# Six of 22 k-pairs by seven products in each down column pair of a decoder layer, not five

## The chip, the cores and the metric

The kernel runs on one core of one Trainium2 chip. The metric is the device time of one execution in microseconds (us). Before the change three runs took 1735.93, 1736.4 and 1738.6 us; the median is 1736.4. Below, PE is the tensor engine, DVE the vector engine, ACT the scalar engine, POOL the GpSimd engine and SP the engine that issues the weight transfers.

## The reference, cut to what matters

One decoder layer over 256 tokens of width 2048 in float32: a feed-forward block (FFN), a mixing block (gated linear attention beside dilated attention), and a second FFN. Nearly all the work is in matrix products with weights.

```python
def swiglu(x, w_gate, w_up, w_down):
    return (jax.nn.silu(x @ w_gate) * (x @ w_up)) @ w_down

x = x + 0.5 * swiglu(rms_norm(x, ffn1_norm), ffn1_w_gate, ffn1_w_up, ffn1_w_down)   # D_FF = 5632
h = rms_norm(x, mix_norm);  z = h @ w_in
...
x = x + jnp.concatenate([o_g, o_a], axis=-1) @ w_out
x = x + 0.5 * swiglu(rms_norm(x, ffn2_norm), ffn2_w_gate, ffn2_w_up, ffn2_w_down)
```

The change concerns the product with `w_down` in both FFNs: 256 tokens by 5632, times 5632 by 2048.

## The kernel before

**Products.** A float32 product is made of three matmuls in a faster format. Each operand is split into a high and a low part (`split`, L111 to L114: ACT copies to the high part `wh`, `hh` or `uh`, DVE subtracts to get `wl`, `hl` or `ul`), and PE adds high by high, high by low and low by high (L274, L276, L278). Stationary is a 128x128 block of activations, moving are 512 columns of weights.

**The down stage.** Its 5632 rows of weights are 44 k-tiles of 128, or 22 k-pairs. Its 2048 columns are two column pairs (`cp` 0 and 1) of 2 x 512. A column pair is one call of `seven_pair`, which walks 22 k-pairs in the order of a string in `DOWN_ORDERS`: `s` is a k-pair done plainly, `g` a k-pair done by seven products. A plain k-pair is two k-tiles x two token halves x two column halves x 3 matmuls = 24 matmuls. A `g` treats token halves, k-tiles and column halves as a 2x2 block product and needs seven block products instead of eight: 21 matmuls (`seven_products`, L298 to L300). `g`s take the k-pairs 0, 1, 2, ... and `s`s the rest. The two FFNs and the gate and up stages before them use the same functions; the last gate and up block, b = 10, is a plain `column_pair`.

**What a `g` needs beside its matmuls.** Of activations: a *form* (`seven_forms`, L316 to L322 and a split), four sums of blocks, made once per FFN and used in both column pairs. Forms lie in parts of `hh` and `hl`, the normed input of the gate and up stages, which are free by then (`dforms`). Of weights: `seven` prepares four parts in order, "plain", "last", "sums" and "more". "plain" first adds rows into `room["sum"]` (L238), which in the down stage is the tile `urs`, and splits the middle of the raw weights. "last" is a half-size split into `hl`. "sums" adds twice in place (L246) and splits `urs`. "more" splits what L246 made, and frees the raw tile.

**Who else uses `urs`.** The gate and up stages end in 11 column blocks; the result of each is transposed in 32x32 pieces by DVE (`us`) and moved by POOL into `urs` in 16 small transfers for each token half (`move_squares`, L133). `finish()` then splits `urs` into `uh` and `ul`, the activations of the down stage. L238 of the first `g` writes `urs`, so it comes behind the `finish()` of block 10.

**Order and buffers.** `weights()` prepares two tiles ahead of PE; there are four `wh`/`wl` buffers and three raw buffers of 1 MB, each filled by one SP transfer. Side work waits in the list `later` and is run a few items a step by `run_later`, spread over `span` steps; a plain k-tile has two steps, a `g` none. The tile framework then orders instructions engine by engine with a schedule of its own; each engine runs its list in order.

**Norm blocks.** `done(t, c, blk)` of the first FFN is `renorm`, which puts into `later` the norm of one block of 512 columns. For c < 2 this is `norm_moved`: DVE transposes, POOL moves 16 pieces into `hh[:, i:i+2]` with i = 8 + 2 * (2 * c + t), and `finish` is held (`held`, `holding`) until the last `g` of the second column pair, because it writes `hh` and `hl` 0 to 7, where forms lie.

Of the kernel before, what the change touches and what calls it, by code (L numbers as in the profile page):

```python
# [38 lines left out]
def _order(text):  # L39

    seven, plain = iter(range(text.count("g"))), iter(range(text.count("g"), len(text)))
    return [(next(seven), True) if c == "g" else (next(plain), False) for c in text]


FF_ORDERS = [_order("ssgssgss" if b in FF_SEVEN else "ssssssss") for b in range(FF // 512)]
DOWN_ORDERS = [_order("ssssssgssgssgssgssgsss"), _order("sgsssgssgsssgssgssssss")]


def layer_kernel(tc, x, xT, gains, gla_gate_up, gla_gate_bias, gla_out_norm, att_q_norm, att_k_norm,
# [6 lines left out]
    with ExitStack() as es:  # L56
# [14 lines left out]
        def four_banks(odd):  # L71

            if odd:
                return [paux.tile([P, 512], F32, name="acc", tag="acc") for _ in range(2)] + [tp_bank() for _ in range(2)]
            return [pacc.tile([P, 512], F32, name="acc", tag="acc") for _ in range(4)]
# [17 lines left out]
        hh = cst.tile([P, KT, S], F32R, name="hh")  # L93
        hl = cst.tile([P, KT, S], F32R, name="hl")
# [66 lines left out]
        def stat_block(t, c):  # L161
            nc.scalar.activation(junk, xs[:, t, c * 512:(c + 1) * 512], AF.Square, accum_out=ss[:, t, c:c + 1])
# [10 lines left out]
        def jobs_of(w, orders):  # L173
            for cp, order in enumerate(orders):
                for kp, seven in order:
                    for part in ("plain", "last", "sums", "more") if seven else (0, 1):
                        yield w, cp * len(order) + kp, part

        jobs = [*jobs_of(w_ff1, FF_ORDERS), *jobs_of(w_dn1, DOWN_ORDERS)]
        jobs += [(w_mix, i, k) for i in range(3 * KT // 2) for k in range(2)] + ["low"]  # L180
        jobs += [(w_mix, i, k) for i in range(3 * KT // 2, 3 * KT) for k in range(2)]
        jobs += [(w_out, i, k) for i in range(w_out.shape[0]) for k in range(2)]
        jobs += [*jobs_of(w_ff2, FF_ORDERS), *jobs_of(w_dn2, DOWN_ORDERS)]

# [69 lines left out]
        def weights(early=False):  # L254
            if early:
                return prepare()
            while jobs and len(ready) <= AHEAD:
                prepare()
            return ready.pop(0)

        def alt(a):

            return a.rearrange("p (b a) -> p a b", b=2)
# [4 lines left out]
        def products(ps, t, acts, ws, first, last, js=((0, 1),)):  # L268
            for jj in js:
                for i, ((ah, al, k), (wh, wl)) in enumerate(zip(acts, ws)):  # L270
                    sh = ah[:, k, t * P:(t + 1) * P]
                    sl = al[:, k, t * P:(t + 1) * P]
                    for j in jj:
                        nc.tensor.matmul(ps[j], lhsT=sh, rhs=alt(wh[:, j, :]), start=first and i == 0, stop=False)  # L274
                    for j in jj:
                        nc.tensor.matmul(ps[j], lhsT=sh, rhs=alt(wl[:, j, :]), start=False, stop=False)  # L276
                    for j in jj:
                        nc.tensor.matmul(ps[j], lhsT=sl, rhs=alt(wh[:, j, :]), start=False, stop=last and i == len(ws) - 1)  # L278

        later = []  # L280
        held, holding = [], [0]

        def run_later(n):
            for _ in range(min(n, len(later))):
                later.pop(0)()

        def seven_products(cs, ms, acts, forms, first, last):

            tok = [slice(t * P, (t + 1) * P) for t in range(NT)]
            a11, a12, a22 = [[a[:, acts[k][2], tok[t]] for a in acts[k][:2]] for t, k in ((0, 0), (0, 1), (1, 1))]
            s1, s3, s2, sa = [[f[:, i, :] for f in forms] for i in range(4)]

            def product(bank, a, ws, j, start, stop):
                nc.tensor.matmul(bank, lhsT=a[0], rhs=alt(ws[0][:, j, :]), start=start, stop=False)  # L298
                nc.tensor.matmul(bank, lhsT=a[0], rhs=alt(ws[1][:, j, :]), start=False, stop=False)  # L299
                nc.tensor.matmul(bank, lhsT=a[1], rhs=alt(ws[0][:, j, :]), start=False, stop=stop)  # L300

            ws = weights()
            product(ms[0], a11, ws, 0, first, last)
            product(cs[0], sa, ws, 1, False, False)
            product(cs[1], a12, weights(), 0, False, False)
            ws = weights()
            product(ms[1], s1, ws, 0, first, last)
            product(ms[3], s3, ws, 1, first, last)
            ws = weights()
            product(ms[2], s2, ws, 0, first, last)  # L310
            product(cs[3], a22, ws, 1, False, False)
# [13 lines left out]
        def seven_pair(acts, pairs, forms, odd, evac, fold, span=None, final=False):  # L325

            cs, ms, folds = four_banks(odd), None, []
            order[0] = 4 * (1 - odd)
            units = [u for kp, seven in pairs for u in ([kp] if seven else [(2 * kp,), (2 * kp + 1,)])]
            lastseven = max(n for n, u in enumerate(units) if not isinstance(u, tuple))  # L330
            steps = span or 2 * sum(isinstance(u, tuple) for u in units)
            total = done = step = n = 0
            while n < len(units):
                u = units[n]
                if isinstance(u, tuple):
                    g = WBUF if final and n == len(units) - WBUF else 1
                    ws = [weights() for _ in range(g)]
                    last = n + g == len(units)
                    for t in range(NT):
                        step += 1  # L340
                        total = max(total, done + len(later))
                        go = min(max(-(-total * min(step, steps) // steps) - done, 0), len(later))
                        done += go
                        run_later(go)
                        if folds:
                            folds.pop(0)()
                        now = [acts[v[0]] for v in units[n:n + g]]
                        products(cs[2 * t:2 * t + 2], t, now, ws, n == 0, last, ((0,), (1,)) if g > 1 else ((0, 1),))
                        if last:
                            evac(t, [c.rearrange("p (a b) -> p b a", b=2) for c in cs[2 * t:2 * t + 2]])  # L350
                    n += g
                    continue
                start = ms is None
                if start:
                    ms = four_banks(1 - odd)
                seven_products(cs, ms, acts[2 * u:2 * u + 2], forms[u], start, n == lastseven)
                if n == lastseven:
                    folds = fold([m.rearrange("p (a b) -> p b a", b=2) for m in ms])
                    if holding[0] == 1:
                        later.extend(held)  # L360
                        held.clear()
                        holding[0] = total = done = step = 0
                        steps = 2 * (len(units) - n) - 6
                n += 1
# [36 lines left out]
        def ffn(name, done, extra=None, final=False):  # L401
            with tc.tile_pool(name=name, bufs=1, reuse_waits="tile") as fp:
# [67 lines left out]
                def lent(a, k, i):  # L470
                    return a[:, k:k + 2, :].rearrange("p k (t q) -> p (k t) q", q=P) if i else a[:, k:k + 2, :].rearrange("p k s -> p (k s)").unsqueeze(1)

                rooms["down"] = {"sum": urs, "wh": lent(hl, 8, 0), "wl": lent(hl, 10, 0)}
                dforms = {kp: [lent(hh, 2 * kp, 1), lent(hl, 2 * kp, 1)] for kp in range(4)}
                dforms[4] = [lent(hl, 12, 1), lent(hl, 14, 1)]
                for kp in range(5):
                    later.insert(min(2 * kp + 1, len(later)), lambda kp=kp: seven_forms(dacts[2 * kp:2 * kp + 2], dforms[kp], t512("full"), t512("sums")))
                for cp in range(2):
                    def evac(t, ps, cp=cp):
# [18 lines left out]
                    holding[0] = NT - cp  # L498
                    seven_pair(dacts, DOWN_ORDERS[cp], dforms, cp, evac, fold, span=28 if cp else 20, final=final and cp == 1)
                spare.close()  # L500
# [23 lines left out]

        def renorm(t, c, gi):

            later.append(lambda: (norm_moved if c < 2 else norm_block)(t, c, gi))
            later.append(lambda: stat_block(t, c))
            if c == 3:
                later.append(lambda: norm_finish(t))  # L530

# [384 lines left out]
```

## Time and profile before

| what | value |
|---|---|
| median of three runs | 1736.4 us |
| the profiled execution, its own time | 1736.26 us |
| its span, first to last instruction | 1734.5 us |
| DVE busy | 1299.5 us (75%) |
| ACT busy | 921.3 us (53%) |
| POOL busy | 438.9 us (25%) |
| mean granted clock | 1.00 |
| weights' transfers of the down stages | 88 of 1 MB, 4.8 us from issue to landing (median) |
| POOL transfers into `urs` | 704 of 16 KB, 3.6 us from issue to landing (median) |

Times in the profile are us from the first instruction. In the first FFN block 10 of the gate and up stage ends on PE at about 457 us and the down stage runs to about 680 us; in the second FFN it runs from about 1509 us to the end. In a timeline row the columns are start, duration, engine, line, operation, what is written <- what is read, count, and in brackets the idle time before it with what ended it.

### The profile page before, as it was taken

What the parts mean: (1) busy time and instruction counts of PE and PEld (TensorE: products, weight loads), DVE (VectorE), ACT (ScalarE), POOL (GpSimd) and SP (SyncE); (2) the same over time, 40 slices, a digit from 0 to 9 for tenths busy, and PEclk for the clock granted to TensorE, in tenths of its full rate; (3) what the DMA queues carried; (4) which work ended last, traced back from release to release, by engine and by line L of the source; (5) the groups of instructions that cost most, each with busy time, mean ns of one, the idle gap of its engine ahead of it and who ended that gap; (6) DMA issues with size and microseconds to landing.
All of it is one profiled execution on the core that took longest, in us unless ns stands there. A gap on an engine that the chain in (4) does not pass through costs nothing.

```text
span 1734.5 us, 22127 instructions
## 1 busy us (share of the span) xinstructions
PE 1725.2 (99%) x8100; PEld 1503.4 (87%) x8100; DVE 1299.5 (75%) x1535; ACT 921.3 (53%) x1142; POOL 438.9 (25%) x870
## 2 busy tenths in 40 slices
PE   9999999999999999999999999999999999999999
PEld 7888888888888888888888888888888888888887
DVE  7788888855788787566655658688888965687875
ACT  7555555544555554565754545455555544455453
POOL 0333334444300601011000033333333343320000
PEclk9999999999999999999999999999999999999999
DMA  8666566666656656555444465556666666655653
GB/s 341 219 221 228 207 215 224 234 221 220 209 201 222 209 216 241 194 195 210 161 170 161 155 207 186 226 209 234 224 225 223 219 216 223 209 211 210 232 213 137
DMA packets 80846, 367.59 MB, mean 212 GB/s; under 512 B 19249, under 2 KB 36657, under 8 KB 38497
## 3 DMA queue, kind: packets, MB, share of 16 engines
q1 hardware_dynamic: 50864, 350.25, 55.9%
q0 software_dynamic: 29152, 14.87, 3.4%
q8 instruction: 63, 1.03, 0.2%
q10 hardware_dynamic: 720, 1.07, 0.2%
q14 instruction: 47, 0.38, 0.1%
HBM read 350.38 MB, written 2.10 MB: 203 GB/s over the span
## 4 chain that ended last, share of the span: by engine, by line
PE 82%; DVE 9%; DMA 5%; issue 2%; ACT 1%; POOL 1%; SPq 0%; DVEq 0%; ACTq 0%
PE acc L276 20%; PE acc L278 20%; PE acc L274 20%; DVE wl L114 4%; DMA raw<-in_w_ff_dram 4%; PE tp L278 3%; PE tp L276 3%; PE tp L274 3%; PE acc L300 2%; PE acc L299 2%; PE acc L298 2%; ACT wh L113 1%; DVE raw L246 1%; DMA urs<-us 1%; DVE t L238 1%
## 5 line engine op out<-in xcount | busy, mean ns | idle before, releaser
L114 DVE TENSOR_TENSOR wl<-raw,wh 128x1024 fp32r<-128x1024 f32 (+1 forms) x658 | 793.3, 1218 | 302.9 <-ACT wh L113 299.4
L113 ACT ACTIVATE wh<-raw 128x1024 fp32r<-128x1024 f32 (+1 forms) x660 | 682.2, 1048 | 562.5 <-PE acc L278 337.0
L133 POOL DMA_DIRECT2D urs<-us x704 | 344.3, 497 | 551.9 <-issue 287.6
L276 PE MATMUL acc<-wl,hh 128*128 128x512 f32 x1376 | 416.6, 381 | 0.4 <-DVE wl L114 0.4
L278 PE MATMUL acc<-wh,hl 128*128 128x512 f32 x1376 | 414.6, 380 | 0.0
L274 PE MATMUL acc<-wh,hh 128*128 128x512 f32 x1376 | 409.2, 381 | 1.6 <-ACT wh L113 1.6
L274 PEld LDWEIGHTS acc<-wh,hh 128*128 128x128 f32 x1376 | 259.5, 189 | 39.3 <-ACT wh L113 2.7
L276 PEld LDWEIGHTS acc<-wl,hh 128*128 128x128 f32 x1376 | 259.4, 189 | 38.6 <-DVE wl L114 1.5
L278 PEld LDWEIGHTS acc<-wh,hl 128*128 128x128 f32 x1376 | 259.6, 189 | 36.5
L276 PE MATMUL acc<-wl,uh 128*128 128x512 f32 x408 | 122.8, 379 | 0.0
L278 PE MATMUL acc<-wh,ul 128*128 128x512 f32 x408 | 122.5, 379 | 0.0
L274 PE MATMUL acc<-wh,uh 128*128 128x512 f32 x408 | 119.6, 379 | 0.2 <-ACT wh L113 0.2
L133 POOL DMA_DIRECT2D hh<-us x128 | 62.2, 508 | 158.9 <-issue 133.5
L274 PEld LDWEIGHTS acc<-wh,uh 128*128 128x128 f32 x408 | 77.0, 189 | 11.6 <-ACT wh L113 0.6
L278 PEld LDWEIGHTS acc<-wh,ul 128*128 128x128 f32 x408 | 77.1, 189 | 11.0
L276 PEld LDWEIGHTS acc<-wl,uh 128*128 128x128 f32 x408 | 77.1, 189 | 10.9
L165 POOL TENSOR_TENSOR rs<-a,mhalf 128x4 f32<-128x4 f32 (+1 forms) x12 | 17.4, 1454 | 256.8 <-DVE a L592 256.8
L274 PE MATMUL tp<-wh,hh 128*128 128x512 f32 x192 | 58.6, 379 | 0.0
L278 PE MATMUL tp<-wh,hl 128*128 128x512 f32 x192 | 57.1, 379 | 0.0
L276 PE MATMUL tp<-wl,hh 128*128 128x512 f32 x192 | 57.1, 379 | 0.0
L238 DVE TENSOR_TENSOR t<-raw 128x1024 f32<-128x1024 f32 x28 | 33.8, 1207 | 25.6 <-DMA raw<-in_w_ff_dram 25.6
L113 ACT ACTIVATE wh<-t 128x1024 fp32r<-128x1024 f32 x28 | 29.5, 1054 | 39.7 <-DVE t L238 33.0
(273 smaller groups left out, 1994.8 us busy)
## 6 DMA issues: line engine op xcount, KB each, us to landing
raw<-in_w_ff_dram SPq DMA_DIRECT2D x175, 1024.0 KB, 5.0
raw<-in_w_dn_dram SPq DMA_DIRECT2D x88, 1024.0 KB, 4.8
raw<-in_w_mix_dram SPq DMA_DIRECT2D x48, 1024.0 KB, 4.7
raw<-in_w_out_dram SPq DMA_DIRECT2D x16, 1024.0 KB, 4.8
urs<-us POOLq DMA_DIRECT2D x704, 16.0 KB, 3.6
xs<-in_x_dram SPq DMA_DIRECT2D x2, 1024.0 KB, 9.7
hh<-us POOLq DMA_DIRECT2D x128, 16.0 KB, 3.4
xt<-in_xT_dram SPq DMA_DIRECT2D x7, 256.0 KB, 6.6
```

The lines of the kernel that those rows point to most:

```text
L113: nc.scalar.activation(dst_h, src, AF.Copy)
L114: nc.vector.tensor_sub(dst_l, src, dst_h.bitcast(F32))
L133: nc.gpsimd.dma_start(dst[32 * q:32 * q + 32, r * P:(r + 1) * P], src[32 * r:32 * r + 32, q * P:(q + 1) * P])
L165: nc.gpsimd.tensor_tensor(dst, src, mhalf[:, :src.shape[-1]], op=ALU.pow)
L238: nc.vector.tensor_add(room["sum"], b1, mid)
L246: nc.vector.tensor_add(raw[:, 1, j, :], b, raw[:, 1, j, :])
L274: nc.tensor.matmul(ps[j], lhsT=sh, rhs=alt(wh[:, j, :]), start=first and i == 0, stop=False)
L276: nc.tensor.matmul(ps[j], lhsT=sh, rhs=alt(wl[:, j, :]), start=False, stop=False)
L278: nc.tensor.matmul(ps[j], lhsT=sl, rhs=alt(wh[:, j, :]), start=False, stop=last and i == len(ws) - 1)
L298: nc.tensor.matmul(bank, lhsT=a[0], rhs=alt(ws[0][:, j, :]), start=start, stop=False)
L299: nc.tensor.matmul(bank, lhsT=a[0], rhs=alt(ws[1][:, j, :]), start=False, stop=False)
L300: nc.tensor.matmul(bank, lhsT=a[1], rhs=alt(ws[0][:, j, :]), start=False, stop=stop)
```

## The change

Each string of `DOWN_ORDERS` gets a sixth `g`. In the first column pair the first `g` moves from the seventh place to the fifth, and the last two `g`s have one `s` between them instead of two. In the second column pair three spacings of two `s`s and one of one `s` follow the first wide one. There is a sixth form; forms 1 to 4 take the room of the old forms 0 to 3, form 5 that of the old form 4, and form 0 lies in `hh` 12 to 15, where `norm_moved` of c = 1 wants to put its moved block. So the norm and statistics blocks of c = 1 go to a list `second` and join `later` only after the first `g` of the second column pair, the last reader of form 0.

```diff
-DOWN_ORDERS = [_order("ssssssgssgssgssgssgsss"), _order("sgsssgssgsssgssgssssss")]
+DOWN_ORDERS = [_order("ssssgssgssgssgssgsgsss"), _order("sgsssgssgssgssgsgsssss")]
...
         later = []
+        second = []
...
                 seven_products(cs, ms, acts[2 * u:2 * u + 2], forms[u], start, n == lastseven)
+                if start:
+                    later.extend(second)
+                    second.clear()
...
-                dforms = {kp: [lent(hh, 2 * kp, 1), lent(hl, 2 * kp, 1)] for kp in range(4)}
-                dforms[4] = [lent(hl, 12, 1), lent(hl, 14, 1)]
-                for kp in range(5):
+                dforms = {kp + 1: [lent(hh, 2 * kp, 1), lent(hl, 2 * kp, 1)] for kp in range(4)}
+                dforms[0] = [lent(hh, 12, 1), lent(hh, 14, 1)]
+                dforms[5] = [lent(hl, 12, 1), lent(hl, 14, 1)]
+                for kp in range(6):
                     later.insert(min(2 * kp + 1, len(later)), lambda kp=kp: seven_forms(...))
...
-            later.append(lambda: (norm_moved if c < 2 else norm_block)(t, c, gi))
-            later.append(lambda: stat_block(t, c))
+            to = second if c == 1 and holding[0] else later
+            to.append(lambda: (norm_moved if c < 2 else norm_block)(t, c, gi))
+            to.append(lambda: stat_block(t, c))
```

Lines from L281 on stand 1 to 6 numbers later in the changed kernel (L316 is L317, L320 L321, and so on); L114, L238 and L246 keep theirs.

How the lists of the engines change is shown at two places. The first is the way into the first `g` of the first column pair in the first FFN. On PE the 24 matmuls of each of two plain k-pairs no longer stand before it. On DVE this stood before; `full`, `sums` and the splits of `sums` belong to forms, `wl` to weight tiles, the `ul` row is the `finish()` of the second token half of block 10, and the row with `urs<-raw` is the first instruction of the `g` that needs `urs`:

```order
L320 TENSOR_TENSOR sums<-full 128x128
L321 SCALAR_TENSOR_TENSOR sums<-sums,full 128x128
L114 TENSOR_TENSOR wl<-raw,wh 128x1024
L322 TENSOR_TENSOR sums<-full,sums 128x128
L114 TENSOR_TENSOR hl<-sums,hh 128x512
L114 TENSOR_TENSOR hl<-sums,hl 128x512
L114 TENSOR_TENSOR ul_2980<-urs,uh_2979 128x4x128
L238 TENSOR_TENSOR urs<-raw 128x1024
L246 TENSOR_TENSOR raw<-urs,raw 128x512
L246 TENSOR_TENSOR raw<-raw 128x512
L114 TENSOR_TENSOR wl<-urs,wh 128x1024
```

And this stands there in the changed kernel:

```order
L317 TENSOR_TENSOR full<-uh,ul 128x256 x2
L321 TENSOR_TENSOR sums<-full 128x128
L320 TENSOR_TENSOR sums<-full 128x128
L114 TENSOR_TENSOR hl<-sums,hh 128x512
L322 SCALAR_TENSOR_TENSOR sums<-sums,full 128x128
L323 TENSOR_TENSOR sums<-full,sums 128x128
L114 TENSOR_TENSOR hl<-sums,hl 128x512
L114 TENSOR_TENSOR ul_2980<-urs,uh_2979 128x4x128
L238 TENSOR_TENSOR urs<-raw 128x1024
L246 TENSOR_TENSOR raw<-urs,raw 128x512
L246 TENSOR_TENSOR raw<-raw 128x512
L114 TENSOR_TENSOR wl<-urs,wh 128x1024
```

The end of the list is the same, `ul`, L238, twice L246, split of `urs`; all six forms still stand ahead of it, and four splits of weight tiles no longer do. On ACT the same place read, before, with `uh` for the two `finish()`es and `wh<-urs` for the part "sums":

```order
L113 ACTIVATE wh<-raw 128x1024 x2
L113 ACTIVATE hh<-sums 128x512
L113 ACTIVATE hl<-raw 128x512
L113 ACTIVATE wh<-raw 128x1024
L113 ACTIVATE uh_2979<-urs 128x4x128
L113 ACTIVATE wh<-raw 128x1024 x2
L113 ACTIVATE hh<-sums 128x512
L113 ACTIVATE hl<-sums 128x512
L113 ACTIVATE uh_2979<-urs 128x4x128
L113 ACTIVATE wh<-urs 128x1024
```

And in the changed kernel:

```order
L113 ACTIVATE wh<-raw 128x1024
L113 ACTIVATE hl<-raw 128x512
L113 ACTIVATE wh<-raw 128x1024 x3
L113 ACTIVATE hh<-sums 128x512 x2
L113 ACTIVATE uh_2979<-urs 128x4x128
L113 ACTIVATE hh<-sums 128x512 x2
L113 ACTIVATE hl<-sums 128x512
L113 ACTIVATE uh_2979<-urs 128x4x128
L113 ACTIVATE wh<-urs 128x1024
```

No weight tile is split any more between the two `finish()`es; the forms and both `finish()`es stand ahead of `wh<-urs`, as they did.

The second place is the last two `g`s of the second column pair in the first FFN. On DVE, before, with `hf` and `hl<-hf` for the held norm blocks:

```order
L238 TENSOR_TENSOR urs<-raw 128x1024
L114 TENSOR_TENSOR wl<-raw,wh 128x1024
L114 TENSOR_TENSOR hl<-raw,hl 128x512
L114 TENSOR_TENSOR hl<-hf,hh 128x4x128
L114 TENSOR_TENSOR wl<-raw,wh 128x1024
L153 TENSOR_TENSOR hf<-hh,gT 128x512
L114 TENSOR_TENSOR wl<-raw,wh 128x1024
L114 TENSOR_TENSOR hl<-hf,hh 128x4x128
L246 TENSOR_TENSOR raw<-urs,raw 128x512
L114 TENSOR_TENSOR wl<-urs,wh 128x1024
L246 TENSOR_TENSOR raw<-raw 128x512
L114 TENSOR_TENSOR wl<-raw,wh 128x1024 x2
```

And in the changed kernel, from the "sums" of the fifth `g` to that of the sixth:

```order
L114 TENSOR_TENSOR wl<-urs,wh 128x1024
L153 TENSOR_TENSOR hf<-hh,gT 128x512
L238 TENSOR_TENSOR urs<-raw 128x1024
L114 TENSOR_TENSOR wl<-raw,wh 128x1024 x3
L114 TENSOR_TENSOR hl<-raw,hl 128x512
L114 TENSOR_TENSOR hl<-hf,hh 128x4x128
L114 TENSOR_TENSOR wl<-raw,wh 128x1024
L114 TENSOR_TENSOR hl<-hf,hh 128x4x128
L246 TENSOR_TENSOR raw<-urs,raw 128x512
L114 TENSOR_TENSOR wl<-urs,wh 128x1024
L246 TENSOR_TENSOR raw<-raw 128x512
L114 TENSOR_TENSOR wl<-raw,wh 128x1024 x2
```

L238 of the sixth `g` now stands ahead of the fifth's last split, and the two last held splits stand inside the sixth `g`.

## The prediction

> **What bounds the kernel now.** I read the page first: busy shares and granted clock.
>
> ```profile
> PE 1725.2 (99%) x8100; PEld 1503.4 (87%) x8100; DVE 1299.5 (75%) x1535; ACT 921.3 (53%) x1142; POOL 438.9 (25%) x870
> PEclk9999999999999999999999999999999999999999
> ```
>
> PE is busy in 1725.2 of 1734.5 us at full clock: every matmul taken away is a gain, and every wait of PE is a loss, one for one. So the second view is the list of what PE waits for (total us, times, longest).
>
> ```profile
> PE acc L274 <- ACT wh L113: 1.9, 2, 1.6
> PE tp L102 <- DVE warm L99: 1.5, 1, 1.5
> PE tp L298 <- ACT wh L113: 0.7, 2, 0.5
> PE acc L298 <- ACT wh L113: 0.6, 1, 0.6
> ```
>
> Nothing else is above 0.4 us. The two largest waits are at the program's start; the L298 rows are `g`s that found their weights up to 0.6 us late. DVE, 75% busy, is the engine that can make PE wait, so the third view is busy time by stretches of the down stage of the first FFN (columns: window, length, PE, PEld, DVE, ACT, POOL, clock, DMA share, GB/s).
>
> ```profile
> 461.10:484.80 23.70, 23.70 (x112) 20.75 (x111) 22.89 (x47) 13.70 (x17) 13.70 (x29) 1.00 0.66 229
> 490.00:577.00 87.00, 87.00 (x404) 75.78 (x402) 71.02 (x76) 46.57 (x54) 6.72 (x14) 1.00 0.59 208
> ```
>
> Ahead of the first `g` DVE is full (22.89 of 23.70 us); behind it, it has 18% in hand. So room for more `g`s is in the second stretch, and the change takes part of it from the first.
>
> **Matmuls removed.** PE's timeline around the first `g` (start, duration, engine, line, what):
>
> ```profile
> 488.37 0.38 PE L298 MATMUL acc<-wh,uh 128*128 128x512 f32 x1
> 490.31 0.38 PE L298 MATMUL acc<-wh,hh 128*128 128x512 f32 x1
> 490.53 0.38 PE L298 MATMUL tp<-wh,hh 128*128 128x512 f32 x1
> 1541.75 0.38 PE L298 MATMUL acc<-wh,hh 128*128 128x512 f32 x1
> ```
>
> From the first row to the third there are ten starts in 2.16 us, 0.216 us each (durations overlap). One more `g` in four column pairs takes away 4 x 3 = 12 matmuls: **-2.59 us**. The two plain k-pairs that no longer stand before the first `g` are 48 matmuls: PE comes to it 10.37 us earlier, in each FFN.
>
> **The first `g` of the first column pair.** Its parts "plain" and "last" could be made earlier, but "sums" splits `urs`, which L238 writes only behind the `finish()` of block 10. When does that come free? On DVE and ACT, where the changed order has the same tail:
>
> ```profile
> 484.83 0.68 DVE L114 TENSOR_TENSOR ul<-urs,uh 128x512 fp32r<-128x512 f32 x1
> 485.55 1.22 DVE L238 TENSOR_TENSOR urs<-raw 128x1024 f32<-128x1024 f32 x1
> 488.15 1.22 DVE L114 TENSOR_TENSOR wl<-urs,wh 128x1024 fp32r<-128x1024 f32 x1
> 489.44 1.22 DVE L114 TENSOR_TENSOR wl<-raw,wh 128x1024 fp32r<-128x1024 f32 x1
> ...
> 484.10 0.61 ACT L113 ACTIVATE uh<-urs 128x512 fp32r<-128x512 f32 x1
> 486.89 1.06 ACT L113 ACTIVATE wh<-urs 128x1024 fp32r<-128x1024 f32 x1 [2.18 <-DVE urs L238]
> ```
>
> From the start of the `ul` split to the end of `wl<-urs` are 489.37 - 484.83 = 4.54 us, a chain in which each step needs the one before. PE needed `wh<-urs` at 490.31 and, four matmuls with `wh` later, `wl<-urs`. So before there were about 2 us in hand; 10.37 us earlier there are none, unless the `ul` split comes earlier too. What stands before it:
>
> ```profile
> L114 DVE TENSOR_TENSOR wl<-raw,wh 128x1024 fp32r<-128x1024 f32 x9 | 11.0, 1221 | 0.1
> L316 DVE TENSOR_TENSOR full<-uh,ul 128x256 f32<-128x256 f32 x10 | 3.8, 416 | 0.1
> L322 DVE TENSOR_TENSOR sums<-full,sums 128x128 f32<-128x128 f32 x5 | 1.4, 290 | 0.1
> L114 DVE TENSOR_TENSOR hl<-sums,hh 128x512 fp32r<-128x512 f32 x4 | 2.7, 686 | 0.0
> ...
> L133 POOL DMA_DIRECT2D urs<-us x32: 496/496/507, 459.2 to 477.8; - x32
> urs<-us POOLq DMA_DIRECT2D x32, 16.0 KB, 3.9
> raw<-in_w_dn_dram SPq DMA_DIRECT2D x6, 1024.0 KB, 5.1
> ```
>
> These are DVE's groups from 461.1 to 486.7 us then POOL's moves of block 10 and the transfers around them (count, size, median us from issue to landing). The order moves four `wl` splits behind the `ul` split (4 x 1.22 = -4.9 us) and adds a sixth form before it (2 x 0.42 + 4 x 0.29 + 0.69 = +2.7 us): DVE alone would allow 484.8 - 2.2 = 482.6. POOL bounds it too: its last move is issued at 477.8 and lands about 3.9 us later, ACT's `uh` takes 0.61: 482.3 at the earliest. POOL's 32 issues of 0.5 us are not shortened by the change. I take 483.3, 0.7 us over DVE's count, because the forms now stand in a row and alternate with ACT; the bounds are 482.3 and 484.8. `wl<-urs` is then ready at 483.3 + 4.54 = 487.8. PE's need of it lies behind the two `wh` matmuls that `wh<-urs` itself lets through, which come about 0.43 us after 490.31: 490.31 + 0.43 - 10.37 = 480.4. (`wh` of "more", which the next two need, is made by ACT at the same time as `wl<-urs`.) **Stall: 7.5 us**, bounds 6.5 (landing) to 9.0 (no time saved on DVE). In the second FFN, by the same rows:
>
> ```profile
> 1536.12 0.69 DVE L114 TENSOR_TENSOR ul<-urs,uh 128x512 fp32r<-128x512 f32 x1
> 1539.44 1.22 DVE L114 TENSOR_TENSOR wl<-urs,wh 128x1024 fp32r<-128x1024 f32 x1
> ```
>
> 1536.1 - 1.5 + 4.54 = 1539.2, need 1541.75 + 0.43 - 10.37 = 1531.8: **7.4 us**, same bounds. The PE queue is in order, so nothing behind the waiting matmul runs; the stall is not made up later, because PE has no idle time to give.
>
> **The clock after the stall.** The trace of before has no PE wait as long as this one. Its nearest rows are the program's start and the one wait of 1.61 us:
>
> ```profile
> 1.49 4.63 PE L102 MATMUL tp<-warm 128*128 128x128 f32 x20 [1.49 <-DVE warm L99]
> 6.34 0.63 PE L276 MATMUL acc<-wl,hh 128*128 128x512 f32 x1
> 6.77 0.63 PE L278 MATMUL acc<-wh,hl 128*128 128x512 f32 x1
> 7.43 0.92 PE L274 MATMUL acc<-wh,hh 128*128 128x512 f32 x3
> 8.18 0.38 PE L276 MATMUL acc<-wl,hh 128*128 128x512 f32 x1
> 13.84 0.48 PE L274 MATMUL acc<-wh,hh 128*128 128x512 f32 x1 [1.61 <-ACT wh L113]
> ```
>
> Before 7.43 us a matmul of this form takes 0.63 us and the next starts 0.43 us later, half the later pace; that lasted from 1.49 to 7.43, and half of these 5.9 us was lost, 2.9 us. After the 1.61 us wait the first matmul took 0.48 us, so the pace was kept. A stall of 7.5 us lies far beyond 1.61 and is more like an idle start, so I take **+2.9 us for each stall**, bounds 0 (as after 1.61) and 2.9.
>
> [...]
>
> **The second column pair.** First, the new wait: norm blocks of c = 1 are put into `later` only after the first `g`. POOL's moves and PE's first `g` of that pair:
>
> ```profile
> 570.28 8.28 POOL L133 DMA_DIRECT2D hh<-us  x17 [91.99 <-issue]
> 580.71 3.89 POOL L133 DMA_DIRECT2D hh<-us  x8 [2.15 <-issue]
> ...
> 577.45 0.70 PE L274 MATMUL acc<-wh,uh 128*128 128x512 f32 x2 [0.25 <-ACT wh L113]
> ```
>
> POOL moves c = 0 until about 579 anyway, and the first `g` has ended when the plain matmul of 577.45 begins, so what is queued behind loses nothing; held splits come tens of us later. I cost it at 0; if the cover were gone, one 8 us of POOL work would shift, with no PE reader before 640 us.
>
> Second, the spacing. In the first FFN the `g`s of this pair share DVE with held splits, and a raw tile frees only when "more" is split:
>
> ```profile
> 594.12 3.71 DVE L114 TENSOR_TENSOR wl<-raw,wh 128x1024 fp32r<-128x1024 f32 x3 [1.21 <-ACT wh L113]
> 600.41 1.23 DVE L238 TENSOR_TENSOR urs<-raw 128x1024 f32<-128x1024 f32 x1 [2.58 <-DMA raw<-in_w_dn_dram]
> 610.40 5.77 DVE L114 TENSOR_TENSOR wl<-raw,wh 128x1024 fp32r<-128x1024 f32 x5 [1.21 <-ACT wh L113]
> ```
>
> From the end of one `g`'s last split (about 595.3) over a transfer (5.1 us, the median row above) to the like split of the next (611.6) go 16.3 us, where a `g` and two plain pairs are 69 x 0.216 = 14.9 us of PE. Before, a wider spacing followed each such round; now three follow each other, then a narrower one. Each round can fall 1.4 us behind, two of them 2.8; but tiles are two ahead (5.2 us). I take **+0.5**, nearest to the present rows with no such PE wait; bounds 0 and 2.8. In the second FFN no norm blocks share DVE: 0. The closer last `g`s of the first pair lie in the stretch with 18% in hand: 0.
>
> **Sum.** 1734.5 - 2.6 + 7.5 + 7.4 + 0.5 + 2 x 2.9 = 1753.1 us of span. The profiled execution took 1736.26 us, 1.8 more than its span and 0.1 under the median of 1736.4; so **1755.0 us**.
>
> **Rivals.**
> - The stall comes, the clock stays (as after 1.61 us): 1755.0 - 5.8 = 1749.2 us.
> - The stall, the clock's fall, and the rounds of the second column pair fall behind by the full 2.8 us or somewhat more: 1757.3 to 1758.
> - The other side: the stall is hidden. This needs the `ul` split at 480.4 - 4.5 = 475.9 or sooner, before POOL's last move is even issued (477.8). It decides once block 10's moves land 6.4 us earlier (475.3 in place of 481.7), which POOL could give only by issuing them without pauses and with landings of the shortest kind: 32 x 0.5 = 16 us from 459.2 is 475.2, before any landing. Then only the matmuls remain: 1736.3 - 2.6 = 1733.7, -0.15%, which is no change by the bound below. For it speaks only that POOL is idle for long before 459.2; against it that the moves wait for the block's last result, whose place is unchanged. A gain over 0.2% isn't in the matmuls, as four times three are all there is.
> - The change doesn't do what it says (no twelve matmuls fewer, or the first `g` not earlier): the order of PE shows both, so little is left for it.
>
> **How the numbers follow.** Chances: forecast 0.50; clock stays 0.30; rounds fall behind too 0.10; hidden 0.07; other 0.03. The range reaches from below the second case, with a stall of 6.5 us each (1749.2 - 1.9 = 1747.3) and a part of the way to the hidden one, 1745, to 1760, which takes in stalls of 9.0 us with half of the clock's loss or the third case with 1 us more per stall. It leaves out the hidden case and the far ends. A measurement can tell about 0.2%, 3.5 us, from no change: slower 0.92, within 0.05, faster 0.03.
>
> **What would show it.** Right: PE's list of waits has two new entries near 480 and 1532 us, each 6.5 to 9 us at L298 or L299 of the first `g` and ended by `wh` or `wl` of L113 or L114; behind each, matmuls of 0.63 us for some us. `wl<-urs` ends near 487.8. Wrong: no such waits; `ul<-urs` of block 10 long before 482; matmuls at 0.38 us right after the wait; or a loss in other places, above all near 611 to 630 us. The second FFN with a much smaller stall than the first would show that held work, not `urs`, is the cause.

## The result, and the profile after

The changed kernel takes 1751.04 us (median of 5 runs, 1750.03 to 1752.78) against 1736.4 us: a ratio of 1.0085, interval 1.0074 to 1.0096. It is slower, as forecast; the forecast of 1755.0 us was 4 us too high, within its range.

The page of the changed kernel, its busy times and PE's list of waits (total us, times, longest):

```profile
span 1749.3 us, 22160 instructions
PE 1727.2 (99%) x8088; PEld 1505.4 (86%) x8088; DVE 1320.6 (75%) x1569; ACT 930.0 (53%) x1152; POOL 440.2 (25%) x870
...
PE acc L299 <- ACT wh L113: 12.5, 2, 6.4
PE acc L274 <- ACT wh L113: 2.2, 2, 2.0
PE tp L102 <- DVE warm L99: 1.5, 1, 1.5
PE tp L299 <- ACT wh L113: 1.3, 4, 0.4
```

The twelve matmuls are gone (8100 to 8088), yet PE is busy 2 us longer, and one entry is new: two waits of 12.5 us together. PE's timeline shows both, with what stands on either side:

```profile
479.77 0.38 PE L301 MATMUL acc<-hl,ul 128*128 128x512 f32 x1
486.19 0.80 PE L299 MATMUL acc<-wh,hh 128*128 128x512 f32 x1 [6.04 <-ACT wh L113]
486.78 0.63 PE L299 MATMUL tp<-wh,hh 128*128 128x512 f32 x1
487.65 0.80 PE L299 MATMUL tp<-wh,hh 128*128 128x512 f32 x1 [0.23 <-ACT wh L113]
488.24 0.64 PE L299 MATMUL acc<-wh,uh 128*128 128x512 f32 x1
488.66 0.63 PE L300 MATMUL acc<-wl,hh 128*128 128x512 f32 x1
...
490.37 1.49 PE L274 MATMUL acc<-wh,uh 128*128 128x512 f32 x3
491.65 0.46 PE L300 MATMUL tp<-wl,hh 128*128 128x512 f32 x1
...
1537.54 0.38 PE L301 MATMUL acc<-hl,ul 128*128 128x512 f32 x1
1544.34 0.80 PE L299 MATMUL acc<-wh,hh 128*128 128x512 f32 x1 [6.42 <-ACT wh L113]
```

In each FFN the wait stands where the first `g` of the first pair needs its "sums". From start to start, 479.77 to 486.19 is 6.4 us where 0.2 would do: 6.2 us lost. ("By starts" below means this: the spacing of matmul starts, less 0.216 us each.) Behind it matmuls take 0.63 us. The busy times by stretches (window, length, PE, PEld, DVE, ACT, POOL, clock, DMA share, GB/s) give the clock:

```profile
480.15:486.19 6.04, 0.00 (x1) 0.00 (x0) 5.21 (x11) 2.24 (x4) 0.00 (x0) 0.90 0.00 0
486.19:491.65 5.46, 5.22 (x11) 3.70 (x12) 4.86 (x5) 3.99 (x4) 0.00 (x0) 0.50 0.32 86
491.65:500.00 8.35, 8.35 (x40) 7.33 (x39) 7.54 (x8) 3.64 (x6) 0.00 (x0) 0.99 0.77 287
```

For 5.46 us PE ran at half clock and started 11 matmuls, which need 2.4 us at full pace: 3.1 us more, 9.3 us in this FFN. In the second FFN it is 6.6 + 3.1 = 9.7 us.

What PE waited for stands in the chain of work that ended last (start, length, what), a piece of which is:

```profile
479.52 0.67 DVE full L317 x2
480.19 0.20 DVE sums L321
480.39 0.20 DVE sums L320
480.59 0.60 DVE hl L114
481.19 0.21 DVE sums L322
481.43 0.30 DVE sums L323
481.76 0.64 ACT hl L113
...
483.03 0.69 DVE ul L114
483.75 1.24 DVE urs L238
485.00 0.70 DVE raw L246
485.73 0.70 DVE raw L246
486.54 1.06 ACT wh L113
```

The sixth form, then the `ul` split of block 10, then L238 and the rest, each behind the one before. The `ul` split starts at 483.03, forecast as 483.3. No transfer from POOL stands in this piece, although the prediction had the landing of POOL's last move as a second bound, 482.3, close by.

### The profile page after: what moved, and what is told of

It reads as the page before. It is cut to its first block, busy times and chain, and to the rows that moved or that the text cites. A ratio compares the mean times of both kernels' runs of the same rounds, so it can differ in the third digit from the quotient of the medians.

```text
span 1749.3 us, 22160 instructions
## 1 busy us (share of the span) xinstructions
PE 1727.2 (99%) x8088; PEld 1505.4 (86%) x8088; DVE 1320.6 (75%) x1569; ACT 930.0 (53%) x1152; POOL 440.2 (25%) x870
## 4 chain that ended last, share of the span: by engine, by line
PE 86%; DVE 6%; DMA 4%; issue 1%; ACT 1%; POOL 1%; DVEq 0%; ACTq 0%; SPq 0%; POOLq 0%
PE acc L274 21%; PE acc L276 20%; PE acc L278 20%; PE tp L278 4%; PE tp L276 4%; PE tp L274 4%; PE acc L301 3%; PE acc L300 3%; PE acc L299 3%; DMA raw<-in_w_ff_dram 2%; DVE wl L114 2%; DMA urs<-us 2%; PE tp L299 1%; PE tp L300 1%; PE tp L301 1%
## 5 line engine op out<-in xcount | busy, mean ns | idle before, releaser
L114 DVE TENSOR_TENSOR wl<-raw,wh 128x1024 fp32r<-128x1024 f32 (+1 forms) x658 | 792.3, 1217 | 296.4 <-ACT wh L113 293.0
L274 PE MATMUL acc<-wh,hh 128*128 128x512 f32 x1376 | 409.3, 381 | 2.1 <-ACT wh L113 2.0
L276 PE MATMUL acc<-wl,uh 128*128 128x512 f32 x384 | 115.7, 379 | 0.0
L278 PE MATMUL acc<-wh,ul 128*128 128x512 f32 x384 | 115.4, 379 | 0.0
L274 PE MATMUL acc<-wh,uh 128*128 128x512 f32 x384 | 113.6, 383 | 0.2 <-ACT wh L113 0.2
L274 PEld LDWEIGHTS acc<-wh,uh 128*128 128x128 f32 x384 | 73.4, 191 | 11.2 <-ACT wh L113 0.6
L278 PEld LDWEIGHTS acc<-wh,ul 128*128 128x128 f32 x384 | 72.6, 189 | 10.3
L276 PEld LDWEIGHTS acc<-wl,uh 128*128 128x128 f32 x384 | 72.6, 189 | 10.2
L238 DVE TENSOR_TENSOR t<-raw 128x1024 f32<-128x1024 f32 x28 | 33.8, 1206 | 23.7 <-DMA raw<-in_w_ff_dram 23.7
L299 PE MATMUL acc<-wh,hh 128*128 128x512 f32 x100 | 38.4, 388 | 12.5 <-ACT wh L113 12.5
```

The lines of the kernel that those rows point to most:

```text
L114: nc.vector.tensor_sub(dst_l, src, dst_h.bitcast(F32))
L238: nc.vector.tensor_add(room["sum"], b1, mid)
```

## The experiments

**Theory**: the first `g` of the first pair comes while `urs` still holds block 10. **Main rival**: DVE has too much to do, with six forms and more `g`s, wherever the first one stands. All experiments are timed against the kernel before, on the same chip.

### One part of the change at a time

e1 keeps the first `g` at the seventh place and has six of them. It leaves out the last of the nine operations of the fold in each first pair, since only eight steps follow its last `g`.

```diff
-DOWN_ORDERS = [_order("ssssgssgssgssgssgsgsss"), _order("sgsssgssgssgssgsgsssss")]
+DOWN_ORDERS = [_order("ssssssgssgssgsgssgsgss"), _order("sgsssgssgssgssgsgsssss")]
```

> Six products by seven in each column pair as in the changed kernel, but the first one of the first pair stays at the seventh place. Theory (the room urs is still held by block 10 when the first g comes): the waits of PE at the first g shrink to at most 2 us each, no matmul runs at 0.63 us behind them, and the time is 1733.8 us (1736.4 - 2.6) to 1737.8. Rival (six forms and closer g's overload DVE, wherever the first g stands): waits of over 4 us stay at the first g or move to a later one, 1743 us or more.

1740.45 us, ratio 1.002 (1.0011 to 1.0029). The long waits are gone and the clock stays at 1.0, but the time is 2.7 us above the theory's upper end, between the two. By starts PE loses 2.0 and 1.6 us at the two first `g`s, as the theory has it, and 2.2 and 1.5 us near 580 and 647 us, in the second pair, which it has not; what made these two stays open. So e8 repeats it with three plain k-pairs behind the last `g`, and every operation of the fold:

```diff
-DOWN_ORDERS = [_order("ssssssgssgssgsgssgsgss"), _order("sgsssgssgssgssgsgsssss")]
+DOWN_ORDERS = [_order("ssssssgssgssgsgsgsgsss"), _order("sgsssgssgssgssgsgsssss")]
```

> First g at the seventh place again, six g's, with three plain k-pairs behind the last one, so that every addition of the fold is made. Theory: waits of at most 2 us at the first g of each FFN, none of over 2 us at the four g's that now alternate with single plain k-pairs, 1736 to 1740 us. Rival (alternating g's are too much for DVE or the transfers): waits of PE between 520 and 560 us, 1742 us or more.

1738.15 us, ratio 1.0008 (1.0000 to 1.0017). Waits at the first `g`s of 2.3 and 1.7 us by starts (at most 2 were expected), none over 0.5 us in the second pair and none at the four `g`s that alternate with single `s`: the rival falls. The matmuls saved are spent on the sixth form, which makes a first `g` late that had some 2 us in hand.

e2 is the reverse: the kernel before with five `g`s and five forms, only the first `g` moved.

```diff
-DOWN_ORDERS = [_order("ssssssgssgssgssgssgsss"), _order("sgsssgssgsssgssgssssss")]
+DOWN_ORDERS = [_order("ssssgssssgssgssgssgsss"), _order("sgsssgssgsssgssgssssss")]
```

> The kernel before, five g's and five forms, with nothing but its first g at the fifth place. Theory (urs): waits of 5 to 6.5 us at the first g of each FFN and 2.9 us of slow clock behind each, nothing saved: 1750 to 1754 us. Rival (the sixth form and the sixth g overload DVE): at most small waits, 1736 to 1741 us.

1751.3 us, ratio 1.0086 (1.0072 to 1.0100): the whole loss without any of the rest. Its timelines of PE and DVE at that place:

```profile
483.77 0.80 PE L298 MATMUL acc<-wh,hh 128*128 128x512 f32 x1 [3.83 <-ACT wh L113]
484.36 0.63 PE L298 MATMUL tp<-wh,hh 128*128 128x512 f32 x1
...
480.61 0.68 DVE L114 TENSOR_TENSOR ul<-urs,uh 128x512 fp32r<-128x512 f32 x1
```

The wait is 3.83 us, not 6.04: with one form less the `ul` split starts at 480.61, 2.4 us earlier. So of the changed kernel's wait about 4 us come from the place and 2.2 from the sixth form. It also shows that POOL's moves had landed by then, against the forecast's bound of 482.3. The expected wait of 5 to 6.5 us was too long. That the time came out right is in part luck: the expected terms add up to 1736.4 + 2 x (5 + 2.9) = 1752.2 us at least, above the lower end of the range. By starts the waits cost 4.0 us each and the slow pace behind them 3.6 and 3.0 us.

e3 is the changed kernel with the first pair's old order, so only the second pair has a sixth `g`.

```diff
-DOWN_ORDERS = [_order("ssssgssgssgssgssgsgsss"), _order("sgsssgssgssgssgsgsssss")]
+DOWN_ORDERS = [_order("ssssssgssgssgssgssgsss"), _order("sgsssgssgssgssgsgsssss")]
```

> The changed kernel with the first column pair's order as before: five g's there, six in the second pair, the sixth form and the late norm blocks kept. Theory (only the first pair's first g costs): 1735.1 us (1736.4 - 1.3), up to 1737 if the sixth form makes the first g late. Rival (the closer g's or the norm blocks that wait in the second pair cost time): 1738 us or more, with waits of PE between 590 and 680 us.

1739.16 us, ratio 1.0016 (1.0007 to 1.0024). Taken by time alone the rival was right; the trace says otherwise. There is no wait of PE between 590 and 680 us, and this stands at the first `g` of the first pair:

```profile
492.93 0.48 PE L299 MATMUL acc<-wh,hh 128*128 128x512 f32 x1 [0.34 <-ACT wh L113]
494.38 0.48 PE L299 MATMUL tp<-wh,hh 128*128 128x512 f32 x1 [0.75 <-ACT wh L113]
...
489.76 0.69 DVE L114 TENSOR_TENSOR ul<-urs,uh 128x512 fp32r<-128x512 f32 x1
```

`ul` comes at 489.76 in place of 484.83. Of these 4.9 us, 2.3 are a later start of everything in this execution (by starts PE lost 6.0 us in its first 19 us, 3.7 in the profile of before; behind a wait of 2.13 us two matmuls took 1.22 us from 16.14 us on, where two took 0.70 in the changed kernel); the other 2.6 are the sixth form. By starts PE loses 1.6 and 1.8 us at the two first `g`s. With six matmuls fewer, 1736.4 - 1.3 + 3.4 = 1738.5. Spacing and late norm blocks cost nothing.

### Take the collision away

e4 leaves order and forms alone and gives block 10 another room: `hh` 8 to 11, which nothing uses between the end of the gate and up stage and the first norm blocks.

```diff
                         ur = urs[:, t, :]
                         squares(us, u)
-                        move_squares(ur, us)
+                        if b == FF // 512 - 1:
+                            ur = hh[:, 8 + 2 * t:10 + 2 * t, :].rearrange("p k s -> p (k s)")
+                            move_squares(ur, us.bitcast(F32R))
+                            ur = ur.bitcast(F32)
+                        else:
+                            move_squares(ur, us)
```

> The changed kernel, order and forms untouched, but the squares of block 10 are moved into hh 8 to 11, not into urs, so that the first g's sums find urs free. Theory (urs): both long waits go, or leave under 1 us each, no slow clock: 1733.8 to 1736 us. Rival (DVE has too much to do ahead of a first g at the fifth place): waits of over 4 us stay and end with DVE or ACT work on weights, 1744 us or more.

1734.46 us, ratio 0.9988 (0.9979 to 0.9997). The waits are gone; PE and DVE at the same place:

```profile
479.11 0.38 PE L301 MATMUL acc<-hl,ul 128*128 128x512 f32 x1
479.32 0.38 PE L299 MATMUL acc<-wh,hh 128*128 128x512 f32 x1
...
464.27 1.22 DVE L238 TENSOR_TENSOR urs<-raw 128x1024 f32<-128x1024 f32 x1
...
473.96 1.22 DVE L114 TENSOR_TENSOR wl<-urs,wh 128x1024 fp32r<-128x1024 f32 x1
...
476.97 0.69 DVE L114 TENSOR_TENSOR ul<-hh,uh 128x512 fp32r<-128x512 f32 x1
```

L238 runs at 464.27 in place of 483.75, and `wl<-urs` is ready 4 us ahead of PE, with the first `g` at the fifth place and all six forms. This decides for `urs` and against DVE's load. The forms are now spread between weight tiles, and only parts of them stand ahead of the "sums".

e9 runs the same kernel again, and e10 gives the kernel before the same room:

> The kernel of e4 once more, for the size of its gain: 12 matmuls fewer and no wait at the first g give 1733.8 us; between 1733 and 1735.5 us.

> The kernel before (five g's, first one at the seventh place), with block 10 moved into hh 8 to 11 as in e4 and nothing else. Theory (the gain of e4 is that of the matmuls, the own room only takes the wait away): no wait there before, so 1736.4 us within 0.1%, 1.5 to 3 us above e9. Rival (the own room is itself a gain): as fast as e9.

e9: 1733.49 us, ratio 0.9982 (0.9973 to 0.9991). e10: 1736.67 us, ratio 1.0004 (0.9995 to 1.0013). The room alone changes nothing; with it the six `g`s bring the 0.15% that twelve matmuls are worth (e9 is 3.2 us under e10, 1.5 to 3 were expected). It beats both kernels.

### The price of the slow clock

e5 and e6 put idle matmuls on PE into the wait: `fill` is 28 or 14 in the first `g` of the first pair and 0 elsewhere.

```diff
             product(cs[1], a12, weights(), 0, False, False)
+            for _ in range(fill):
+                nc.tensor.matmul(ms[1], lhsT=a11[0], rhs=alt(ws[0][:, 0, :]), start=True, stop=True)
             ws = weights()
```

> The changed kernel with 28 idle matmuls (6.0 us at full pace; they write a bank that the next product clears) on PE between the parts "last" and "sums" of the first g of the first pair, in both FFNs: PE waits as long for urs, but busy. Theory (an idle PE of 6.2 and 6.6 us loses half its pace for the next 5.4 us): no matmul of 0.63 us behind the g, and 2 x 2.9 us less: 1745 us. Rival (the slow pace comes from something else at that place): 1751 us, with matmuls of 0.63 us as before.

1748.87 us, ratio 1.0073 (1.0060 to 1.0085). By stretches (columns as above):

```profile
481.43:487.64 6.21, 6.21 (x29) 5.10 (x27) 5.38 (x11) 2.41 (x4) 0.00 (x0) 1.00 0.00 0
487.64:491.15 3.51, 2.75 (x13) 2.11 (x13) 3.44 (x4) 3.16 (x4) 0.00 (x0) 1.00 0.00 0
```

The clock stays at 1.00 here, so the slow pace came from idling. But the saving is 2.2 us by the medians, not 5.8. The second row says why: at full pace the 11 starts that took 5.46 us take 3.51 us, of which 1.1 us is a further wait, for `wh` of "more". At half pace that wait was mostly covered. So the slow clock costs 5.46 - 3.51 = 1.95 us net in this FFN; twice that is 3.9. The profiled spans differ by only 2.2 (1749.3 and 1747.1), mostly because e5 lost 1.6 us more in its first 19 us, where its clock was at half from 15.72 to 19.13 us, behind a wait of 1.9 us; the two ratios with their intervals leave room for 3.9. The wait at full pace is 6.2 + 1.1 = 7.3 us.

> The same with 14 idle matmuls (3.0 us), so that PE is idle for 3.2 and 3.5 us only. If any idle time beyond some 2 us costs the pace (4.0 us did): 1751 us, with matmuls of 0.63 us behind. [...]

1752.66 us, ratio 1.0096 (1.0080 to 1.0111): the pace is lost all the same. Both FFNs by stretches, the idle time first:

```profile
482.87:485.89 3.02, 0.01 (x1) 0.00 (x0) 2.92 (x4) 1.06 (x1) 0.00 (x0) 1.00 0.00 0
485.89:487.35 1.46, 0.70 (x2) 0.30 (x3) 1.39 (x3) 1.11 (x2) 0.00 (x0) 0.80 0.00 0
487.35:490.78 3.43, 3.43 (x9) 2.81 (x10) 3.43 (x3) 2.30 (x3) 0.00 (x0) 0.59 0.36 60
1541.24:1544.26 3.02, 0.00 (x0) 0.00 (x1) 2.92 (x4) 1.06 (x1) 0.00 (x0) 1.00 0.00 0
1544.26:1545.71 1.45, 0.70 (x2) 0.30 (x2) 1.38 (x3) 1.11 (x2) 0.00 (x0) 0.72 0.00 0
1545.71:1551.80 6.09, 6.09 (x15) 4.88 (x16) 4.76 (x5) 2.96 (x4) 0.00 (x0) 0.51 0.63 218
```

Right behind 3.0 us of idling the clock is still full; it falls in the 1.5 us behind, which hold two matmuls and a second wait, and slow matmuls follow for 3.4 and 6.1 us. The time is near the 1751 us expected if idle time beyond some 2 us costs the pace: this length of idling saves nothing.

e7 has six `g`s, the first at the sixth place.

```diff
-DOWN_ORDERS = [_order("ssssgssgssgssgssgsgsss"), _order("sgsssgssgssgssgsgsssss")]
+DOWN_ORDERS = [_order("sssssgssgssgsgssgsgsss"), _order("sgsssgssgssgssgsgsssss")]
```

> Six products by seven in each pair, the first of the first pair at the sixth place, between the changed kernel (fifth place: 6.2 and 6.6 us of waiting) and the seventh place (about 1.5 us). Theory (urs comes free at a time of its own, and every place is 5.2 us of PE against 2.3 us of DVE): waits of 3 to 4 us, so 1740 to 1742 us if the pace is kept behind them and up to 1747 if it is lost. Rival (a wait that does not depend on the place): 1738 us or less, or 1750 or more.

1745.72 us, ratio 1.0054 (1.0041 to 1.0066). The wait is 2.86 us (3 to 4 were expected), in both FFNs, with 0.76 behind it, and the clock falls:

```profile
485.17:488.03 2.86, 0.00 (x1) 0.00 (x1) 2.76 (x4) 1.06 (x1) 0.00 (x0) 1.00 0.00 0
488.03:489.49 1.46, 0.70 (x3) 0.30 (x3) 1.39 (x3) 1.11 (x2) 0.00 (x0) 0.94 0.00 0
489.49:493.11 3.62, 3.62 (x9) 2.94 (x10) 3.47 (x3) 2.50 (x3) 0.00 (x0) 0.55 0.31 88
```

Fifth, sixth and seventh place give first waits of 6.0, 2.9 and about 1 us (e8). The time is the theory's, at the end where the pace is lost.

## Why the prediction was right, and what it mis-sized

- **Twelve matmuls, -2.59 us**: right; e9 against e10 shows 3.2 us, with intervals that leave room for it.
- **The first `g` meets `urs`**: right in place, cause and size (e2, e4). Forecast were 7.5 and 7.4 us; e5 shows 7.3 for the first FFN at full pace. The `ul` split was forecast 0.3 us late, and the wait for "more" was counted into the 4.54 us.
- **The bound by POOL's landings, 482.3**: wrong. It took the median landing for the last move; in e2 `ul` ran at 480.61. The forms set the time, as the chain shows. This didn't move the sum, since DVE's count was taken.
- **The clock, 2 x 2.9 us**: right that it falls, mis-sized. PE worked at half pace for 5.46 us, close to the 5.9 taken from the program's start. But the step "half of these was lost" counted it on top of the whole wait, while slow matmuls cover a part of that wait: 1.95 us net in the first FFN. Wait and slow clock together cost 9.3 and 9.7 us, where 10.4 and 10.3 were forecast.
- **The second pair, +0.5 us**: nothing; the longest wait of PE there is 0.16 us, near 586. The late norm blocks cost nothing either.
- **Not counted**: in the rest of the program PE lost 1.6 us less by starts than in the profile of before, in small waits: 0.8 us less near 1276, 0.4 near 1072 and 0.3 near 577, but 0.3 more near 265. The experiments show no cause for that. These terms together, 1.7 + 0.5 + 1.6, are the 3.8 us by which the span of 1753.1 was missed; all three went the same way, so the forecast owes nothing to errors that cancel.
- **The rivals**: "the clock stays" would have given 1749.2, within 2 us of the result, though the clock did fall. The time alone would have chosen the wrong case.

## What to carry to other kernels

Before moving a consumer earlier, list every buffer that it writes, not only what it reads: here the first step of the `g` wrote a room that another stage held, and a room of its own turned a loss of 0.85% into the gain meant. Work added ahead of such a hand-over lengthens the wait, here the sixth form by 2.2 us, although its engine, DVE, was busy only 75% of the span. Price a stall of the tensor engine with the slow clock behind it, even a stall of 2 us, which cost the clock here in two executions (2.13 us in e3, 1.9 in e5) and not in two others (2.02 in the changed kernel, 1.9 in e1); but count the slow matmuls against any wait that they cover.

## What was not expected of the hardware

The length of a wait did not tell here whether PE kept its full clock. Near 14 us, waits of 2.13 (e3) and 1.9 us (e5) were followed by half pace, while after 2.02 (the changed kernel) and 1.9 us (e1) the full pace was kept. In the two long waits of the changed kernel the clock was still full after 4.83 and 5.19 us of idling, and in e6 after 3.02 us. The first four rows are of the changed kernel, the last of e5 (columns as above):

```profile
480.15:484.98 4.83, 0.00 (x1) 0.00 (x0) 4.06 (x9) 1.18 (x3) 0.00 (x0) 1.00 0.00 0
484.98:491.81 6.83, 5.38 (x12) 3.86 (x13) 6.12 (x7) 5.07 (x5) 0.00 (x0) 0.50 0.27 77
1537.92:1543.11 5.19, 0.00 (x1) 0.00 (x0) 4.42 (x10) 1.56 (x3) 0.00 (x0) 1.00 0.00 0
1543.11:1549.94 6.83, 5.37 (x12) 3.83 (x13) 6.11 (x8) 5.07 (x5) 0.00 (x0) 0.50 0.23 80
...
15.72:19.13 3.41, 3.41 (x10) 2.66 (x9) 3.41 (x6) 3.22 (x6) 0.00 (x0) 0.50 1.05 410
```

So the changed kernel ran at half clock from 484.98 to 491.81 and from 1543.11 to 1549.94 us, of which the first 1.2 us each still belonged to the wait. What decides when the clock falls was not shown: no run tests it.

Filling half of the wait (e6) saved nothing. The execution's own start varied: in their first 19 us PE lost 3.3 (e4) to 6.0 us (e3) by starts, a spread as large as the 2.6 us that this change can gain.
